# A two-layer encoder on one core: four plain columns and nine pairs in the later feed-forwards, low halves by adding transfers

## The chip, the core and the metric

The kernel runs on one core of a Trainium2 chip. The metric is the time of one execution in device microseconds, as the median of several runs. A core has a matrix engine (TensorE, PE in the rows; PEld is its weight load), a vector engine (VectorE, DVE), an activation engine (ScalarE, ACT), a general engine (GpSimd, POOL) and a sequencer that issues transfers (SyncE, SP). PE writes its sums to PSUM banks; the other engines work on SBUF, and DVE and ACT also read PSUM.

## The reference

Two layers work on 512 tokens of width 1024, in float32. Each layer has a half-step feed-forward, a mixer (a bidirectional state-space scan in the first layer, neighbourhood attention in the second), a second half-step feed-forward, and a gated embedding. So there are four feed-forwards, and they are where the change is:

```python
def swiglu(x, w_gu, w_down):
    g, u = jnp.split(x @ w_gu, 2, axis=-1)
    return (jax.nn.silu(g) * u) @ w_down

for i in range(DEPTH):                       # 2
    h = h + 0.5 * swiglu(rmsnorm(h, ffn1_norm[i]), ffn1_w_gu[i], ffn1_w_down[i])
    ...                                      # h = h + mixer(rmsnorm(h))
    h = h + 0.5 * swiglu(rmsnorm(h, ffn2_norm[i]), ffn2_w_gu[i], ffn2_w_down[i])
    gate = jax.nn.sigmoid(rmsnorm(h, ple_norm[i]) @ ple_w_gate[i])
    h = h + gate * rmsnorm(p[i] @ ple_w_proj[i], ple_post_norm[i])
```

D_MODEL is 1024 and D_FF 2816, which is 22 columns of 128.

## The kernel before

**Two halves per operand.** PE multiplies operands of a shorter float32 format (float32r). Every float32 operand is therefore split into a high half, which is a rounded copy, and a low half, which is the rest, and each product is three matmuls: high by high (L268, or L483 in a pair), high weight by low activation (L271, L484) and low weight by high activation (L272, L485). A weight unit of 128 by 1024 is loaded by SP into a buffer `wr` (L201) and split by `split_raw`: ACT copies it to `wh` (L218), DVE subtracts that copy from it into `wl` (L220). There are four `wr` buffers and three each of `wh` and `wl`. Activations are split in the same way (L286 and L287, with the norm's gain L289 and L290).

**The order of the weights.** `plan` writes out, for the whole program, in which order units are loaded, combined and split. Its items are "u" (a unit that is split as loaded), "g" and "s" (four blocks of a pair are taken, and sums of them are formed by DVE, L240 to L251) and "o" (one of the pair's seven operands is split). `unit` hands PE the next split unit and first tops up the stock to three, so a unit is prepared two units ahead of its use. The framework orders each engine's instructions by a planner of its own; every engine runs its queue in order.

**A feed-forward.** `ffn_order` gives the order of its work. The gate and up projections of the 22 columns come in two kinds. A *plain* column (`gate_up`) is two units, gate and up, each 24 matmuls over all 512 tokens. The other columns come in *pairs* (`block`): for two columns, the two halves of the tokens and two halves of the input width, seven products take the place of eight (a scheme of the Strassen and Winograd kind), each product 24 matmuls over 256 columns. Their activation operands are sums and differences of parts of the normalised input, which `sums` forms in four steps, kk = 0 to 3, each a run of DVE operations (L437 to L468) with copies by ACT between them. These sums need the norm's factor `R`, which is there during the second plain column (in the first feed-forward the third), so they are formed while PE works on the plain columns. The first product reads a part of all four steps, the second needs all four in full. `activate` turns the two PSUM results of a plain column into an entry of `mids`: DVE multiplies both by the factor (L415, L418), ACT applies silu (L416), POOL multiplies (L419), ACT and DVE split (L286, L287).

The columns are grouped in chunks: before, (0, 6) is plain, and (6, 10), (10, 14), (14, 18), (18, 22) are two pairs each. The down projection of a chunk, eight units, is spread between the products of the chunk after it; L546 adds its result to the residual. In the second feed-forward of a layer, the projection of the embedding (`ple_proj`, two units of `w_proj`) stands between the last product and the last chunk's down units, and the gate (`ple`, eight units of `w_gate`) follows.

**Places.** `sums` is called from the loop at the end of `ffn`, after `gate_up`, one step per plain column up to column 3, and the rest at column 4. The first product of the first feed-forward stands at 74.89 us of the span, that of the second at 989.6. POOL issues no transfer in the kernel before.

Of the kernel before, what the change touches and what calls it, by code (L numbers as in the profile page):

```python
# [14 lines left out]
P = 128  # L15
# [32 lines left out]

def ffn_order():

    for f in range(PLAIN):
        yield "plain", f
    for c in range(1, len(CHUNKS)):
        a, b = CHUNKS[c]
        blocks = [(p, i) for p in range(a // 2, b // 2) for i in range(7)]
        d = 0
        for n, (p, i) in enumerate(blocks):
            yield "block", p, i  # L60
            while d < KD and (d + 0.5) * len(blocks) <= KD * (n + 1):
                yield "down", c - 1, d
                d += 1
    yield "between",
    for d in range(KD):
        yield "down", len(CHUNKS) - 1, d


@with_exitstack
def trunk(ctx, tc, A, out):  # L70
# [72 lines left out]
    def plan():  # L143
# [3 lines left out]
        for i in range(stop):  # L147
            l, w = divmod(i, 4)
            if w in (0, 2):
                gu, gw, dn = [A[f"w_{x}{1 + w // 2}"][l] for x in ("gu", "gw", "dn")]  # L150

                def ahead(p, i_):
                    if i_ == 0:
                        yield "g", [gw[p - PLAIN // 2, x, y] for x, y in ((1, 0), (0, 0), (1, 1), (0, 1))]
                    yield "s", (p, i_)

                for what, *a in ffn_order():
                    if what == "plain":
                        for x in range(2):
                            yield "u", gu[a[0], x]  # L160
                            n = 2 * a[0] + x - (2 * PLAIN - 3)
                            if n >= 0:
                                yield from ahead(PLAIN // 2, n)
                    elif what == "block":
                        yield "o", a
                        if a[1] >= 4 and a[0] < NF // 2 - 1:
                            yield from ahead(a[0] + 1, a[1] - 4)
                    elif what == "down":
                        b = CHUNKS[a[0]]
                        yield "u", dn[a[1], :, b[0] * P:b[1] * P]  # L170
                    elif w == 2:
                        for n in range(2):
                            yield "u", A["w_proj"][l, n]
            elif w == 3:
                for n in range(KD):
                    yield "u", A["w_gate"][l, n]
            elif l % 2 == 0:
# [5 lines left out]
            else:  # L183
# [6 lines left out]

    loads = [x for what, a in todo if what in "gu"
             for x in (zip(a, ("wr", "wr", "md", "md")) if what == "g" else [(a, "wr")])]
# [4 lines left out]
    def load_unit():  # L197
# [3 lines left out]
        sy.dma_start(out=raw[:, :n], in_=src)  # L201
        raws.append((raw, n, tag))
        waiting[tag] += 1

    def take():
        if not raws:
            load_unit()
        raw, n, tag = raws.pop(0)
        waiting[tag] -= 1
        return raw, n  # L210

# [3 lines left out]

    def split_raw(raw, n):
        hi = wp.tile([P, 1024], F32R, name=nm("wh"), tag="wh", bufs=3)
        splits.append(s.copy(out=hi[:, :n], in_=raw[:, :n]))  # L218
        lo = wp.tile([P, 1024], F32R, name=nm("wl"), tag="wl", bufs=3)
        v.tensor_sub(out=lo[:, :n], in0=raw[:, :n], in1=hi[:, :n])  # L220
        ready.append((hi, lo))
# [4 lines left out]
    def prep_next():  # L226
# [3 lines left out]
        what, a = item  # L230
        if what == "u":
            split_raw(*take())
        elif what == "g":
            group[:] = [take()[0] for _ in range(4)]
# [141 lines left out]
    def ffn(norm, nxt, between=None, first=None):  # L376
# [150 lines left out]
        made, left = None, [0, 1, 2, 3]  # L527
        for what, *a in ffn_order():
            if what == "plain":
                gate_up(a[0])  # L530
                while left and R[0] is not None:
                    sums(left.pop(0))
                    if a[0] < 4:
                        break
            elif what == "block":
                if between and a == [CHUNKS[-1][0] // 2, 0]:
                    next(between)
# [3 lines left out]
            else:  # L541
                c, d = a
                last = c == len(CHUNKS) - 1
                pt = mm_bank() if last else px_bank()
                gemm(pt, unit(), [mids[f] for f in range(*CHUNKS[c])])
                v.scalar_tensor_tensor(out=h[d], in0=pt, scalar=0.5, in1=h[d], op0=ALU.mult, op1=ALU.add)  # L546
# [754 lines left out]
def prepare(inp):  # L1301
# [11 lines left out]
    for i in (1, 2):  # L1313
        gu = f[f"ffn{i}_w_gu"]
        gu = np.stack([units(gu[l]).reshape(2, NF, P, 1024).transpose(1, 0, 2, 3) for l in range(DEPTH)])
        o[f"w_gu{i}"] = gu[:, :PLAIN]

        gw = gu[:, PLAIN:].reshape(DEPTH, (NF - PLAIN) // 2, 2, 2, P, 2, 512).transpose(0, 1, 3, 5, 4, 2, 6)
        o[f"w_gw{i}"] = gw.reshape(DEPTH, (NF - PLAIN) // 2, 2, 2, P, 1024)
        o[f"w_dn{i}"] = np.stack([units(f[f"ffn{i}_w_down"][l]) for l in range(DEPTH)])  # L1320
    o["w_gate"] = np.stack([units(f["ple_w_gate"][l]) for l in range(DEPTH)])
# [76 lines left out]
```

## Time and profile before

| | |
|---|---|
| median of 3 runs | 2351.93 us (2351.7 to 2353.02) |
| the profiled execution | 2352.96 us, of which the profile's span is 2351.2 us |
| granted PE clock, mean | 0.997 |
| DMA | 265.95 MB, mean 113 GB/s |
| HBM read, written | 253.40 MB, 10.26 MB |

A row of a timeline gives start and duration in us, the engine, the line, the operation, the buffer written and those read, the shape, how many are merged into the row, and in brackets the idle time before it with what ended it. A row of a group view gives line, engine, operation and buffers, the count, then busy us and mean ns of one, then the idle time of the engine just before these instructions with what ended most of it. A row of a line's own view gives the least, median and greatest duration in ns. A row of the transfers gives buffers, issuing queue, count, size and median us from issue to landing. A matmul's row starts when PE takes it; its duration overlaps with the next one's, so PE's time is read from the distance of starts, and the same holds in part for DVE and ACT.

### The profile page before, as it was taken

What the parts mean: (1) busy time and instruction counts of PE and PEld (TensorE: products, weight loads), DVE (VectorE), ACT (ScalarE), POOL (GpSimd) and SP (SyncE); (2) the same over time, 40 slices, a digit from 0 to 9 for tenths busy, and PEclk for the clock granted to TensorE, in tenths of its full rate; (3) what the DMA queues carried; (4) which work ended last, traced back from release to release, by engine and by line L of the source; (5) the groups of instructions that cost most, each with busy time, mean ns of one, the idle gap of its engine ahead of it and who ended that gap; (6) DMA issues with size and microseconds to landing.
All of it is one profiled execution on the core that took longest, in us unless ns stands there. A gap on an engine that the chain in (4) does not pass through costs nothing.

```text
span 2351.2 us, 35169 instructions
## 1 busy us (share of the span) xinstructions
PE 2327.4 (99%) x13810; PEld 2026.6 (86%) x13810; DVE 1805.7 (77%) x2565; ACT 1111.8 (47%) x1819; POOL 353.7 (15%) x309
## 2 busy tenths in 40 slices
PE   9999999999999999999999999999999999999998
PEld 8899998888888888899997889999877888999987
DVE  7878868877777747978877897887778757777767
ACT  5433445755655653433345443334437744334353
POOL 1000001444445551100003110000100011000020
PEclk9999999999999999999999999999999999999999
DMA  5233324544444543323322332332433233333222
GB/s 191 84 101 104 108 72 131 172 138 138 143 136 142 162 162 107 115 84 104 108 86 84 103 115 85 104 108 77 145 121 130 103 100 100 111 108 99 81 81 81
DMA packets 99238, 265.95 MB, mean 113 GB/s; under 512 B 12016, under 2 KB 12912, under 8 KB 99072
## 3 DMA queue, kind: packets, MB, share of 16 engines
q1 hardware_dynamic: 98784, 263.57, 34.8%
q8 instruction: 108, 1.77, 0.3%
q14 instruction: 58, 0.48, 0.1%
q10 hardware_dynamic: 288, 0.14, 0.0%
HBM read 253.40 MB, written 10.26 MB: 112 GB/s over the span
## 4 chain that ended last, share of the span: by engine, by line
PE 90%; DVE 5%; ACT 1%; issue 1%; POOL 1%; DMA 1%; SPq 0%; POOLq 0%; ACTq 0%; DVEq 0%
PE ps L268 19%; PE ps L271 19%; PE ps L272 19%; PE ps L485 9%; PE ps L484 9%; PE ps L483 9%; PE ps L866 1%; DVE wl L220 1%; PE ps L844 1%; PE ps L887 1%; PE ps L800 1%; PE ps L786 1%; PE ps L1172 1%; DVE md L290 1%; DVE md L287 1%
## 5 line engine op out<-in xcount | busy, mean ns | idle before, releaser
L268 PE MATMUL ps<-md,wh 128*128 128x512 f32 x2128 | 838.4, 395 | 2.7 <-ACT md L286 2.1
L272 PE MATMUL ps<-md,wl 128*128 128x512 f32 x2128 | 830.7, 391 | 4.7 <-DVE wl L220 4.7
L271 PE MATMUL ps<-md,wh 128*128 128x512 f32 x2128 | 831.3, 391 | 0.7 <-DVE md L290 0.5
L218 ACT CAST wh<-wr 128x1024 fp32r<-128x1024 f32 (+2 forms) x401 | 358.1, 894 | 521.4 <-PE ps L271 199.9
L220 DVE TENSOR_TENSOR wl<-wr,wh 128x1024 fp32r<-128x1024 f32 (+2 forms) x401 | 429.0, 1070 | 114.1 <-ACT wh L218 85.3
L272 PEld LDWEIGHTS ps<-md,wl 128*128 128x128 f32 x2128 | 400.1, 188 | 90.7 <-DVE wl L220 6.7
L268 PEld LDWEIGHTS ps<-md,wh 128*128 128x128 f32 x2128 | 400.5, 188 | 84.4 <-issue 3.5
L271 PEld LDWEIGHTS ps<-md,wh 128*128 128x128 f32 x2128 | 400.9, 188 | 81.1 <-issue 3.3
L314 POOL TENSOR_TENSOR sq<-sq,sq 128x512 f32<-128x512 f32 x71 | 101.1, 1424 | 1444.8 <-ACT sq L310 1444.0
L218 ACT CAST wh<-md 128x1024 fp32r<-128x1024 f32 x160 | 167.7, 1048 | 297.8 <-PE ps L484 263.0
L483 PE MATMUL ps<-sc,wh 128*128 128x256 f32 x896 | 253.8, 283 | 4.2 <-ACT wh L218 4.2
L485 PE MATMUL ps<-sc,wl 128*128 128x256 f32 x896 | 254.3, 284 | 0.8 <-DVE wl L220 0.8
L484 PE MATMUL ps<-md,wh 128*128 128x256 f32 x896 | 254.1, 284 | 0.0
L485 PE MATMUL ps<-md,wl 128*128 128x256 f32 x896 | 254.1, 284 | 0.0
L484 PE MATMUL ps<-sc,wh 128*128 128x256 f32 x896 | 254.1, 284 | 0.0
L483 PE MATMUL ps<-md,wh 128*128 128x256 f32 x896 | 253.9, 283 | 0.0
L489 DVE TENSOR_TENSOR t<-ps,t 128x512 f32<-128x512 f32 x224 | 151.7, 689 | 129.8 <-PE ps L485 127.9
L220 DVE TENSOR_TENSOR wl<-md,wh 128x1024 fp32r<-128x1024 f32 x160 | 196.5, 1228 | 26.8 <-ACT wh L218 26.7
L483 PEld LDWEIGHTS ps<-sc,wh 128*128 128x128 f32 x896 | 172.1, 192 | 8.4 <-ACT wh L218 4.6
L484 PEld LDWEIGHTS ps<-sc,wh 128*128 128x128 f32 x896 | 172.2, 192 | 3.7
L484 PEld LDWEIGHTS ps<-md,wh 128*128 128x128 f32 x896 | 172.4, 192 | 1.2
L483 PEld LDWEIGHTS ps<-md,wh 128*128 128x128 f32 x896 | 172.4, 192 | 1.2
(207 smaller groups left out, 2859.8 us busy)
## 6 DMA issues: line engine op xcount, KB each, us to landing
wr<-in_w_in_dram SPq DMA_DIRECT2D x65, 512.0 KB, 3.5
wr<-in_w_gw_dram SPq DMA_DIRECT2D x64, 512.0 KB, 4.1
md<-in_w_gw_dram SPq DMA_DIRECT2D x64, 512.0 KB, 5.0
wr<-in_w_dn_dram SPq DMA_DIRECT2D x128, 256.0 KB, 2.7
wr<-in_w_gu_dram SPq DMA_DIRECT2D x44, 512.0 KB, 3.5
hs<-crow SPq DMA_DIRECT2D x64, 256.0 KB, 3.9
wr<-in_w_dn_dram SPq DMA_DIRECT2D x32, 384.0 KB, 3.1
wr<-in_w_qkv_dram SPq DMA_DIRECT2D x24, 512.0 KB, 3.7
```

Of the source, the lines that this page charges most:

```text
L218: splits.append(s.copy(out=hi[:, :n], in_=raw[:, :n]))
L220: v.tensor_sub(out=lo[:, :n], in0=raw[:, :n], in1=hi[:, :n])
L268: m = te.matmul(out=pt, lhsT=hi[:, sl], rhs=part(xp, 0, cols), start=first and k == 0, stop=False)
L271: te.matmul(out=pt, lhsT=hi[:, sl], rhs=part(xp, 1, cols), start=False, stop=False)
L272: te.matmul(out=pt, lhsT=lo[:, sl], rhs=part(xp, 0, cols), start=False, stop=last and k == n - 1)
L287: v.tensor_sub(out=dst[:, 1, :], in0=src, in1=dst[:, 0, :])
L290: v.scalar_tensor_tensor(out=dst[:, 1, :], in0=src, scalar=gain, in1=dst[:, 0, :], op0=ALU.mult, op1=ALU.subtract)
L314: (v if fast else g).tensor_add(out=self.acc, in0=self.acc, in1=q)
L483: te.matmul(out=o, lhsT=hi[:, sl], rhs=xh, start=j == 0 and kk == 0, stop=False)
L484: te.matmul(out=o, lhsT=hi[:, sl], rhs=xl, start=False, stop=False)
L485: te.matmul(out=o, lhsT=lo[:, sl], rhs=xh, start=False, stop=j == 1 and kk == 3)
L489: v.tensor_add(out=k[to], in0=pt, in1=k[other])
```

## The change

The second, third and fourth feed-forwards get their own list of chunks: four plain columns instead of six, then a chunk of three pairs, (4, 10), and the same last three chunks. So each of them has nine pairs instead of eight. The first feed-forward keeps its list. The weights are laid out on the host to match, one array per feed-forward.

`sums` moves: in the later feed-forwards step 0 follows column 1, steps 1 and 2 follow column 2, and step 3 follows column 3, the last. In the first feed-forward there is one step per column from column 2 on, so that step 3 follows column 5, the last, where it stood after column 4.

Plain units, the two units of the projection and the eight of the gate become items "a". Their high half is made as before. Their low half is no longer a subtraction on DVE: ACT writes the negated, rounded copy into `wl` (a second pass over the raw unit), and a transfer issued by POOL reads the unit once more from its array and adds it to `wl`. Units of the down projections, of the mixers and the products of the pairs are split as before.

```diff
-CHUNKS = ((0, 6), (6, 10), (10, 14), (14, 18), (18, 22))
-PLAIN = CHUNKS[0][1]
+FIRST = ((0, 6), (6, 10), (10, 14), (14, 18), (18, 22))
+OTHERS = ((0, 4), (4, 10), (10, 14), (14, 18), (18, 22))
...
                     if what == "plain":
                         for x in range(2):
-                            yield "u", gu[a[0], x]
-                            n = 2 * a[0] + x - (2 * PLAIN - 3)
+                            yield "a", gu[a[0], x]
+                            n = 2 * a[0] + x - (2 * plain - 3)
...
-                            yield "u", A["w_proj"][l, n]
+                            yield "a", A["w_proj"][l, n]
...
-                    yield "u", A["w_gate"][l, n]
+                    yield "a", A["w_gate"][l, n]
...
-    def split_raw(raw, n):
+    def split_raw(raw, n, src=None):
         hi = wp.tile([P, 1024], F32R, name=nm("wh"), tag="wh", bufs=3)
         splits.append(s.copy(out=hi[:, :n], in_=raw[:, :n]))
         lo = wp.tile([P, 1024], F32R, name=nm("wl"), tag="wl", bufs=3)
-        v.tensor_sub(out=lo[:, :n], in0=raw[:, :n], in1=hi[:, :n])
+        if src is None:
+            v.tensor_sub(out=lo[:, :n], in0=raw[:, :n], in1=hi[:, :n])
+        else:
+            s.activation(out=lo[:, :n], in_=raw[:, :n], func=AF.Copy, scale=-1.0)
+            g.dma_start(out=lo[:, :n], in_=src, accum_op=ALU.add)
         ready.append((hi, lo))
...
-        for what, *a in ffn_order():
+        chunks = FIRST if first else OTHERS
+        for what, *a in ffn_order(chunks):
             if what == "plain":
                 gate_up(a[0])
-                while left and R[0] is not None:
+                n = 1 if first else min(a[0], 2)
+                while left and R[0] is not None and n:
                     sums(left.pop(0))
-                    if a[0] < 4:
-                        break
+                    n -= a[0] < chunks[0][1] - 1
```

More of the change, by code (lines that the diff above doesn't have):

```diff
@@ L65, in ffn_order @@
     for d in range(KD):
[L66 removed]
+        yield "down", len(chunks) - 1, d
 @with_exitstack
@@ L189, in trunk @@
     todo = list(plan())
-    loads = [x for what, a in todo if what in "gu"
+    loads = [x for what, a in todo if what in "agu"
              for x in (zip(a, ("wr", "wr", "md", "md")) if what == "g" else [(a, "wr")])]
@@ L1314, in prepare @@
         gu = f[f"ffn{i}_w_gu"]
[L1315 to L1320, printed above, removed]
+        for l in range(DEPTH):
+            k = 2 * l + i - 1
+            plain = (OTHERS if k else FIRST)[0][1]
+            g_ = units(gu[l]).reshape(2, NF, P, 1024).transpose(1, 0, 2, 3)
+            o[f"w_gu{k}"] = g_[:plain]
+            gw = g_[plain:].reshape((NF - plain) // 2, 2, 2, P, 2, 512).transpose(0, 2, 4, 3, 1, 5)
+            o[f"w_gw{k}"] = gw.reshape((NF - plain) // 2, 2, 2, P, 1024)
+            o[f"w_dn{k}"] = units(f[f"ffn{i}_w_down"][l])
     o["w_gate"] = np.stack([units(f["ple_w_gate"][l]) for l in range(DEPTH)])
```

36 lines of the change are left out of this document (20 added, 16 removed).

## The prediction

> **What bounds the kernel now.** I read the page first (engine shares and the chain that ended last), then the busy time of each engine in the stages that the diff touches, then the timelines of PE, DVE, ACT and POOL there, and last the DMA issues.
>
> ```profile
> PE 2327.4 (99%) x13810; PEld 2026.6 (86%) x13810; DVE 1805.7 (77%) x2565; ACT 1111.8 (47%) x1819; POOL 353.7 (15%) x309
> ...
> PE 90%; DVE 5%; ACT 1%; issue 1%; POOL 1%; DMA 1%; SPq 0%; POOLq 0%; ACTq 0%; DVEq 0%
> ```
>
> PE carries the chain for 90% of the span, so what the change takes from PE is worth its full size only where nothing else becomes late. The 77% of DVE is a mean; in the plain stage of the second feed-forward (940 to 990) and in the first one's (44 to 82) it is another engine:
>
> ```profile
> core 0 of [0], span 2351.2 us
> ...
> 940.00:990.00 50.00, 50.00 (x228) 41.56 (x227) 45.70 (x67) 24.61 (x37) 7.80 (x5) 1.00 0.35 115
> 44.00:82.00 38.00, 33.00 (x144) 26.64 (x143) 37.58 (x57) 18.22 (x30) 6.14 (x4) 0.97 0.24 77
> ```
>
> The columns are the stretch, its length, then busy PE, weight load, DVE, ACT, POOL. DVE is busy 45.70 of 50 and 37.58 of 38 us. In the first feed-forward PE already waits for it (33.00 of 38); in the second PE is full, by a hair, as the next part shows.
>
> **The swap on PE.** Two rows one unit apart for each kind of unit, in the second feed-forward:
>
> ```profile
> 946.11 0.39 PE L268 MATMUL ps<-md,wh 128*128 128x512 f32 x1
> ...
> 951.55 0.39 PE L268 MATMUL ps<-md,wh 128*128 128x512 f32 x1
> ```
> ```profile
> 989.63 0.28 PE L483 MATMUL ps<-sc,wh 128*128 128x256 f32 x1
> ...
> 992.51 0.40 PE L268 MATMUL ps<-md,wh 128*128 128x512 f32 x1
> ```
>
> A plain unit is 24 matmuls over 512 columns: 951.55 - 946.11 = 5.44 us. A product of a pair is 24 over 256: 992.51 - 989.63 = 2.88 us. Two plain columns are four units, 21.76 us; a pair is seven products, 20.16 us. Each of the three later feed-forwards swaps one for the other: -1.60 us each, -4.8 us in all. The down units keep their 22 columns of matmuls, the SP queue keeps its number of loads (four per pair as per two columns), and so neither is charged.
>
> **The cover that goes with it.** The three later feed-forwards lose 21.76 us of plain matmuls behind which DVE forms the operand sums (`sums`, four times) that the products read. What DVE does there:
>
> ```profile
> 952.06 1.22 DVE L220 TENSOR_TENSOR wl<-wr,wh 128x1024 fp32r<-128x1024 f32 x1
> 953.20 0.41 DVE L465 TENSOR_TENSOR t<-t,t 128x256 f32<-128x256 f32 x1
> ```
> ```profile
> 979.90 0.69 DVE L415 TENSOR_TENSOR t<-ps,rt 128x512 f32<-128x512 f32 x1
> 980.50 0.68 DVE L418 TENSOR_TENSOR t<-ps,rt 128x512 f32<-128x512 f32 x1
> ```
> ```profile
> 989.22 0.68 DVE L468 TENSOR_TENSOR md<-t,md 128x512 fp32r<-128x512 f32 x1
> ```
> ```profile
> L220 DVE TENSOR_TENSOR wl<-wr,wh 128x1024 fp32r<-128x1024 f32 (+1 forms) x9 | 10.7, 1189 | 2.1 <-PE ps L338 2.1
> ...
> L287 DVE TENSOR_TENSOR md<-t,md 128x512 fp32r<-128x512 f32 x9 | 6.1, 686 | 2.0 <-ACT md L286 1.6
> ...
> L418 DVE TENSOR_TENSOR t<-ps,rt 128x512 f32<-128x512 f32 x5 | 3.4, 688 | 1.5 <-PE ps L272 1.5
> ```
> ```profile
> L437 DVE SCALAR_TENSOR_TENSOR t<-hs,cst,rt x32: 736/746/1792, 44.2 to 1993.7; 128x512 f32<-128x512 f32 x32
> ```
> ```profile
> 981.44 1.55 POOL L419 TENSOR_TENSOR t<-t,t 128x512 f32<-128x512 f32 x1 [10.86 <-ACT t L416]
> ```
>
> The last operation of the last sums starts at 989.22, and PE begins its products at 989.63: no slack. Now the same stage after the change. One L220 costs DVE 953.20 - 952.06 = 1.14 us from start to start, one 512-wide operation 980.50 - 979.90 = 0.60 us. The group view (941.9 to 989.9, the row of nine L220) holds seven of plain units, one of the first product and one of a down unit; the seven go to the transfers: -7 x 1.14 = -8.0 us. The activation of the fifth column (number 4) goes: three 512-wide operations, -1.8 us, and with it one overlap with POOL: of L437's least, median and greatest 736, 746 and 1792 ns the greatest is the one that runs beside POOL's operation (row at 981.44), so -1.0 us. (Number 5's lay behind the sums.) Added ahead of the last sums is the second product's L220, +1.14 us, because with six columns in the second chunk the first down unit comes after two products instead of one. DVE ends the sums at 989.8 - 8.0 - 1.8 - 1.0 + 1.1 = 980.1. PE comes to the first product at 989.63 - 21.76 = 967.9, and to the second product's fourth operand, which needs the last sums, at 967.9 + 2.88 + 9 x 0.12 = 971.8 (0.12 = 2.88 / 24). PE waits 980.1 - 971.8 = 8.3 us. With the swap, 8.3 - 1.6 = +6.7 us in each, +20 us for three.
>
> The ends of this term: of DVE's idle time in that window, 2.0 + 1.5 = 3.5 us by the group rows could be filled by sums moved ahead (the 2.1 before L220 lie before the norm's factor is there), which leaves a stall of 4.8 and +3.2 each. The program does hoist: in the first feed-forward an L437 of the sums ran ahead of the splits that were written before it.
>
> ```profile
> 44.23 1.78 DVE L437 SCALAR_TENSOR_TENSOR t<-hs,cst,rt 128x512 f32<-128x512 f32 x1
> 46.15 2.39 DVE L287 TENSOR_TENSOR md<-t,md 128x512 fp32r<-128x512 f32 x2
> ```
>
> ```profile
> 1243.97 1.05 ACT L218 CAST wh<-wr 128x1024 fp32r<-128x1024 f32 x1 [2.36 <-PE ps L484]
> ...
> 1250.02 1.14 ACT L286 CAST md<-sq 128x512 fp32r<-128x512 f32 x2
> ```
>
> Upward, ACT gets a second pass per plain unit (1.05 us, row at 1243.97; the row at 1250.02 is used further down) ahead of the copies that the sums wait for, and the L220 that filled DVE's waits inside the sums are gone: four of 1 us, so +10.7 each. Part of the idle time filled and part of this lost, about even, leaves 6.7.
>
> The trace shows no transfer issued by POOL, so what that does to DVE is unknown. [...]
>
> **The adding transfers.** 52 units take them: 8 in the first feed-forward (12 less the four begun by hand), 8 in each other, 4 of the projection, 16 of the gate. Each takes 1.14 us from DVE and gives ACT one more pass, POOL an issue, and the DMA engines 512 KB more.
>
> ```profile
> wr<-in_w_gu_dram SPq DMA_DIRECT2D x44, 512.0 KB, 3.5
> t<-ydram SPq DMA_DIRECT2D x6, 256.0 KB, 6.5
> ```
>
> A low half is now ready after ACT's copy, ACT's negated copy, the issue and the landing: 1.05 + 1.05 + an issue between nothing and 1.6 (one POOL operation in front, the row at 981.44) + a landing between 3.5 and 6.5, the fastest load of that size and the slowest landing of the table: 5.6 to 10.2 us. I take 1 and 5, 8.1 us, the middle of both, since a landing that also adds is nearer to neither row. Its time is two units of PE, 10.88 us, as three low-half buffers allow. So inside the plain units it is hidden behind PE's matmuls; uncovered it would cost up to 10.2. The new waits: ACT's negated copy waits for the buffer, with the gate's activations and the copies of the sums queued behind it, for which DVE waits; POOL's issue waits for that copy, with the next product of L419 behind it, for which ACT and then DVE wait. Both stand in the +10.7. [...]
>
> The first feed-forward keeps its six columns and only gains the transfers:
>
> ```profile
> 79.94 0.58 PE L483 MATMUL ps<-sc,wh 128*128 128x256 f32 x1 [4.19 <-ACT wh L218]
> ...
> 81.55 0.58 PE L485 MATMUL ps<-sc,wl 128*128 128x256 f32 x1 [0.82 <-DVE wl L220]
> ```
> ```profile
> L220 DVE TENSOR_TENSOR wl<-wr,wh 128x1024 fp32r<-128x1024 f32 x5 | 6.1, 1217 | 0.0
> ```
>
> PE stands 4.19 + 0.82 = 5.0 us (the brackets are the idle time before the row). Of the five L220 in that window one is the first product's; four go, 4.6 us of a DVE that has no idle time: -4.5 us. Ends: -5.0 (all) and +0.5, if the last sums, which now stand behind column 5, are kept there.
>
> At the projection and the gate the lead is shorter:
>
> ```profile
> 1250.68 0.50 PE L268 MATMUL ps<-md,wh 128*128 128x512 f32 x1 [1.05 <-ACT md L286]
> ```
> ```profile
> 1287.15 0.50 PE L272 MATMUL ps<-md,wl 128*128 128x512 f32 x1 [2.04 <-DVE wl L220]
> ```
> ```profile
> 1281.85 1.99 ACT L218 CAST wh<-wr 128x1024 fp32r<-128x1024 f32 x2
> ```
>
> Projection: the first low half is there at 1243.97 + 8.1 = 1252.1, wanted at about 1251.1 (two matmuls after 1250.68), and L286, for which PE waits, stands behind two more ACT passes: +1.5 us, from 0 to +3.2 (landing 6.5). Gate: 1281.85 + 8.1 = 1290.0 against 1287.15 is +2.8, less what the freed L220 give back to DVE behind it, at most the 2.0 us of the present stall: +1 us, from -2.0 to +5. Two of each: +5 us.
>
> **Sum.** 20 - 4.5 + 5 = +20.5 us. The profiled execution is 2352.96 us (span 2351.2), 1.0 above the median of 2351.93; the difference set on the median gives 2372.
>
> **Rivals.** *Faster: the sums fit.* The 3.5 us of DVE's idle time are filled, the first down unit (12 matmuls of 0.227, 2.7 us) is put ahead of the second product, and the sums run clear of POOL, which is worth another 1.0 us in each of the two overlaps left: 8.3 - 3.5 - 2.7 - 2.0 = 0.1, and nothing waits. Then -4.8 - 5.0 and at best 2 x -2.0 at the gate: -14 us, 2338. The hoisted L437 speaks for it; against it the L418 row, five activations whose 1.5 us of waiting for PE was not filled by sums. It decides from a stall under 1.6 us. *Slower still: the transfers are late.* If a landing takes 11 us, the chain is 14.1 and a unit comes every (14.1 + 5.44) / 3 = 6.5 us instead of 5.44: +1.07 us for the 24 units of the first feed-forward and the gate, +26 us on top, 2398; in the other three it hides in the stall for the sums. It decides from a landing of 7.8 us. [...] *No change:* stalls of 3 us each (+4 in all), -4.5 and nothing at projection and gate: 2352.
>
> **Numbers.** This kernel can be told from no change at about 0.2%, 4.7 us. Forecast 2372 (from 2357 to 2392 on its own): 0.56; late transfers 0.14; sums fit 0.21; no change 0.09. Faster 0.21, same 0.09, slower 0.70. The range leaves out the tail of each end rival: 2341 to 2399.
>
> **What would show it.** L268 and its two fellows fall by 96 matmuls each, the three 256-wide lines rise by 168 each. PE should show a wait of 4 to 12 us at the first two products of the last three feed-forwards, released by DVE's L468 or L220 or by ACT, and DVE busy without a gap there; the wait in the first feed-forward about 1 us. Wrong if no wait stands there (DVE then started the sums before 946), if plain units wait for the transfer, or if the adding transfers land over 7.8 us after issue.

## The result and the profile after

The changed kernel takes 2393.07 us (median of four, 2389.58 to 2394.76) against 2351.9 us: ratio 1.0172, 95% interval 1.0155 to 1.019. That is slower by 41 us, where 20 were forecast: the sign was right, the size was half. The profiled execution is 2391.99 us, its span 2390.2.

The page of the kernel after: the engines, two DMA queues (packets, MB, share of 16 engines' span), and four rows of the issues (last column: us from issue to landing):

```profile
PE 2335.6 (98%) x14026; PEld 2040.7 (85%) x14026; DVE 1783.6 (75%) x2549; ACT 1171.0 (49%) x1883; POOL 386.4 (16%) x355
...
q1 hardware_dynamic: 98784, 263.57, 33.9%
q0 software_dynamic: 7488, 27.27, 6.4%
...
wr<-in_w_gu_dram SPq DMA_DIRECT2D x32, 512.0 KB, 5.0
wl<-in_w_gu_dram POOLq DMA_DIRECT2D x32, 512.0 KB, 8.0
...
wl<-in_w_gate_dram POOLq DMA_DIRECT2D x16, 512.0 KB, 7.6
...
wl<-in_w_proj_dram POOLq DMA_DIRECT2D x4, 512.0 KB, 6.6
```

DVE's busy time fell by 22 us (from 1805.7) and PE's rose by 8; neither is 41 us. The adding transfers land 6.6 to 8.0 us after their issue (the medians of the three arrays; single ones take 5.5 to 12.1), where 3.5 to 6.5 had been allowed. What PE waited for (us in total, times, longest):

```profile
PE ps L492 <- ACT md L455: 14.8, 4, 4.6
PE ps L281 <- DMA wl<-in_w_gate_dram: 14.3, 3, 6.7
PE ps L281 <- DMA wl<-in_w_gu_dram: 7.0, 4, 3.3
PE ps L281 <- DMA wl<-in_w_proj_dram: 4.4, 2, 2.4
PE ps L494 <- DVE wl L224: 4.0, 6, 1.2
```

Two families stand there. The first and the last row are the products waiting for the sums and for the low halves of their own weights, which DVE forms between the sums (L492 to L494 are the pair's three matmul lines, L455 a copy in `sums`, L224 is before's L220): forecast. The three in the middle are low halves that a transfer had not yet landed (25.7 us): forecast as hidden in the plain columns and as 5 us at projection and gate. Of the 25.7 us, 16.7 stand at the first unit of the projection and of the gate (2.0, 2.4, 6.7 and 5.6), and 9.0 in five waits further on: at the second and fourth unit of a feed-forward, the fifth transfer of the first one and the gate's last unit. The products' wait in the second feed-forward:

```profile
969.59 0.38 PE L494 MATMUL ps<-sc,wl 128*128 128x256 f32 x1 [1.16 <-DVE wl L224]
...
971.67 0.39 PE L494 MATMUL ps<-sc,wl 128*128 128x256 f32 x1 [0.28 <-DVE wl L224]
...
977.34 0.58 PE L492 MATMUL ps<-md,wh 128*128 128x256 f32 x1 [4.57 <-ACT md L455]
978.09 0.58 PE L493 MATMUL ps<-md,wh 128*128 128x256 f32 x1 [0.17 <-DVE md L456]
...
978.68 0.41 PE L492 MATMUL ps<-sc,wh 128*128 128x256 f32 x1
978.90 0.41 PE L493 MATMUL ps<-sc,wh 128*128 128x256 f32 x1
...
984.17 0.28 PE L493 MATMUL ps<-sc,wh 128*128 128x256 f32 x1
984.29 0.28 PE L494 MATMUL ps<-sc,wl 128*128 128x256 f32 x1
```

By the brackets PE stands 6.2 us; by the distance of starts, less a matmul's own time, 7.1. Then something that the prediction has no term for: the rows at 978.68 and 978.90 stand 0.22 us apart, those at 984.17 and 984.29 0.12. After the wait PE runs at half its clock. The windows show it (PEclk is the third number from the end):

```profile
940.00:990.00 50.00, 43.82 (x207) 37.12 (x206) 41.50 (x63) 21.82 (x34) 7.12 (x6) 0.90 0.40 103
44.00:82.00 38.00, 35.76 (x165) 29.03 (x164) 34.92 (x54) 21.89 (x34) 10.49 (x9) 1.00 0.70 188
968.00:985.00 17.00, 10.82 (x55) 9.41 (x54) 15.00 (x24) 6.76 (x12) 1.58 (x1) 0.80 0.29 105
```

In the first row PE is busy 43.82 of 50 us (50.00 before) at a clock of 0.90 (1.00), and DVE 41.50 (45.70); in the third, around the wait, the clock is 0.80. In the second, the first feed-forward, PE went from 33.00 to 35.76 of 38 us. The trace's record of the granted clock has seven stretches at 0.50, each 3.41 or 6.83 us long, which begin inside a wait or less than 1 us behind it. The length of the wait does not settle it alone: two of them follow waits of 1.9 and 3.3 us, and beside the projection's waits of 2.0 and 2.4 us the clock stayed at 1.00.

A table of stages shows where the 39 us of the span (2390.2 - 2351.2) lie. Each number is how much more (us) a stage took than in the kernel before, read from the timelines between the same instructions: the norm's first small matmul at a stage's start, and the last DVE operation of the second chunk's down units (L556) at the end of a feed-forward's part. "Gate" runs from there to the next norm, or to the end, and so holds what the entry to the third feed-forward costs too. The other kernels are those of the experiments.

| stage | after | transfers only | columns only | no add | entries on DVE | entries, six columns | entries, early down | columns, filled |
|---|---|---|---|---|---|---|---|---|
| feed-forward 1 | -5.4 | -2.7 | -1.9 | -6.4 | -3.2 | -3.6 | -4.7 | -2.0 |
| mixer | +0.4 | -0.6 | +1.7 | -0.9 | -0.6 | -0.7 | -0.4 | +1.8 |
| feed-forward 2 | +13.6 | +5.1 | +9.4 | +8.8 | +9.6 | +4.5 | +4.8 | +8.4 |
| gate, entry to 3 | +8.8 | +8.8 | +0.1 | +1.3 | +0.8 | +2.3 | +0.9 | 0.0 |
| feed-forward 3 | +7.3 | +5.8 | +10.3 | +8.0 | +11.9 | +4.4 | +10.0 | +8.5 |
| mixer | -0.5 | -0.8 | -0.8 | -0.5 | -0.8 | -0.8 | -0.8 | -0.8 |
| feed-forward 4 | +10.3 | +3.7 | +9.4 | +7.9 | +13.6 | +6.8 | +4.7 | +8.4 |
| gate | +4.5 | +8.1 | -0.1 | 0.0 | +0.2 | +0.2 | +0.2 | -0.1 |
| span | +39.0 | +27.4 | +28.1 | +18.1 | +31.5 | +13.1 | +14.6 | +24.2 |

My theory from this: three costs add up. The sums come late in the later feed-forwards (as forecast), PE loses its clock after these waits, and the adding transfers land too late wherever a stage begins. The rivals: one of the two edits does all the damage; the half clock is only a sign of the waits and costs nothing itself; every adding transfer is late, not only those at a stage's entry; and what is slow in the transfers is POOL's issue, not the add.

### The profile page after: what moved, and what is told of

The parts are those of the page before. It is cut to its first block, busy times and chain, and to the rows that moved or that the text cites. A ratio compares the mean times of both kernels' runs of the same rounds, so it can differ in the third digit from the quotient of the medians.

```text
span 2390.2 us, 35793 instructions
## 1 busy us (share of the span) xinstructions
PE 2335.6 (98%) x14026; PEld 2040.7 (85%) x14026; DVE 1783.6 (75%) x2549; ACT 1171.0 (49%) x1883; POOL 386.4 (16%) x355
## 5 line engine op out<-in xcount | busy, mean ns | idle before, releaser
L281 PE MATMUL ps<-md,wl 128*128 128x512 f32 (+1 forms) x2032 | 797.0, 392 | 26.4 <-DMA wl<-in_w_gate_dram 14.3
L277 PE MATMUL ps<-md,wh 128*128 128x512 f32 (+1 forms) x2032 | 804.2, 396 | 0.0
L280 PE MATMUL ps<-md,wh 128*128 128x512 f32 (+1 forms) x2032 | 795.2, 391 | 0.0
L281 PEld LDWEIGHTS ps<-md,wl 128*128 128x128 f32 x2032 | 383.5, 189 | 112.2 <-DMA wl<-in_w_gate_dram 15.6
L277 PEld LDWEIGHTS ps<-md,wh 128*128 128x128 f32 x2032 | 384.2, 189 | 77.0 <-issue 3.5
L280 PEld LDWEIGHTS ps<-md,wh 128*128 128x128 f32 x2032 | 384.0, 189 | 75.6 <-issue 3.3
L224 DVE TENSOR_TENSOR wl<-wr,wh 128x1024 fp32r<-128x1024 f32 (+2 forms) x343 | 355.9, 1038 | 104.9 <-ACT wh L221 80.7
L492 PE MATMUL ps<-md,wh 128*128 128x256 f32 x980 | 279.3, 285 | 14.8 <-ACT md L455 14.8
L494 PE MATMUL ps<-sc,wl 128*128 128x256 f32 x980 | 279.2, 285 | 4.0 <-DVE wl L224 4.0
L493 PE MATMUL ps<-md,wh 128*128 128x256 f32 x980 | 279.3, 285 | 0.5 <-DVE md L456 0.5
L494 PE MATMUL ps<-md,wl 128*128 128x256 f32 x980 | 278.8, 284 | 0.0
L493 PE MATMUL ps<-sc,wh 128*128 128x256 f32 x980 | 278.6, 284 | 0.0
L492 PE MATMUL ps<-sc,wh 128*128 128x256 f32 x980 | 278.2, 284 | 0.0
L224 DVE TENSOR_TENSOR wl<-md,wh 128x1024 fp32r<-128x1024 f32 x175 | 213.6, 1221 | 21.4 <-ACT wh L221 21.3
L492 PEld LDWEIGHTS ps<-md,wh 128*128 128x128 f32 x980 | 189.5, 193 | 17.2 <-ACT md L455 15.9
L494 PEld LDWEIGHTS ps<-sc,wl 128*128 128x128 f32 x980 | 189.1, 193 | 6.0 <-DVE wl L224 6.0
L492 PEld LDWEIGHTS ps<-sc,wh 128*128 128x128 f32 x980 | 189.3, 193 | 3.6
L493 PEld LDWEIGHTS ps<-sc,wh 128*128 128x128 f32 x980 | 189.1, 193 | 3.6
```

What stands on the lines that cost most here:

```text
L277: m = te.matmul(out=pt, lhsT=hi[:, sl], rhs=part(xp, 0, cols), start=first and k == 0, stop=False)
L280: te.matmul(out=pt, lhsT=hi[:, sl], rhs=part(xp, 1, cols), start=False, stop=False)
L281: te.matmul(out=pt, lhsT=lo[:, sl], rhs=part(xp, 0, cols), start=False, stop=last and k == n - 1)
L492: te.matmul(out=o, lhsT=hi[:, sl], rhs=xh, start=j == 0 and kk == 0, stop=False)
L493: te.matmul(out=o, lhsT=hi[:, sl], rhs=xl, start=False, stop=False)
L494: te.matmul(out=o, lhsT=lo[:, sl], rhs=xh, start=False, stop=j == 1 and kk == 3)
```

## The experiments

The kernel before ran beside all of them: 2353.27 us beside the transfers, the columns, the spare matmuls in the changed kernel and the first feed-forward alone; 2352.74 beside the two kernels with entries on DVE and the two with an earlier down unit; 2352.76 beside the other four. Kernels with the transfers vary by 3 to 10 us between runs, so their differences are read by stages too.

**Transfers only.** Six plain columns everywhere, sums in their old places; the low halves by adding transfers (64 of them, since the later feed-forwards have twelve plain units again, where the changed kernel has 52).

```diff
-OTHERS = ((0, 4), (4, 10), (10, 14), (14, 18), (18, 22))
+OTHERS = FIRST
...
-                n = 1 if first else min(a[0], 2)
-                while left and R[0] is not None and n:
+                while left and R[0] is not None:
                     sums(left.pop(0))
-                    n -= a[0] < chunks[0][1] - 1
+                    if a[0] < 4:
+                        break
```

> The kernel before with adding transfers for all plain units, the projection and the gate, but six plain columns and the old places of the sums everywhere. Theory A (three causes add up: the sums come late in the three later feed-forwards, low halves land late where the lead is short, and after every longer wait PE runs at half its clock for 3.4 to 6.8 us): the first feed-forward keeps its gain of about 5, the gates cost 4 to 5 each, the first plain units of the later feed-forwards 2 to 5 each, so 10 to 18 us over before, 2362 to 2370. Rival B (the four columns are the whole loss, the transfers are harmless): 5 to 6 us under before, 2346. Rival C (the transfers are nearly the whole loss): 30 us or more over before.

Measured: 2383.01 us (2380.47 to 2385.7), ratio 1.0126 (1.0113 to 1.014): +30 us, above the 2362 to 2370 that my theory gave. PE's waits:

```profile
PE ps L281 <- DMA wl<-in_w_gate_dram: 14.9, 3, 6.6
PE ps L281 <- DMA wl<-in_w_gu_dram: 11.9, 7, 3.2
```

Nothing else waits for as much. The transfers alone, put where DVE's subtraction did no harm, cost as much as three quarters of the whole loss; a kernel with the old columns and the old cover still pays for them.

**Columns only.** The new columns and the sums' new places, the low halves by DVE as before.

```diff
         if what == "a":
-            split_raw(*take())
+            split_raw(*take()[:2])
```

> The changed kernel with every low half formed by the subtraction on DVE again, four columns and nine pairs kept. Theory A: no wait for a transfer, but three or four more subtractions of 1.14 us lie ahead of the last sums: waits of 10 to 12 us in front of the products and about 3 us of half clock behind them, less 1.6 for the swap, 11 to 14 us in each of three, so 2386 to 2394. Rival B: the same or more than the changed kernel, 2393 and up. Rival C: under 2367, since the columns cost little by themselves.

Measured: 2382.06 us (2378.96 to 2383.51), ratio 1.012 (1.0107 to 1.0134): +29 us, 9.4 to 10.3 in each later feed-forward, nothing at the gates; 11 to 14 each had been expected. Each part alone is slower by about 30 us and both together by 41. Two reasons are likely, and no run separates them: the waits for low halves partly fall into time in which DVE's late sums would have held PE anyway, and the transfers take seven subtractions from DVE in each of these stages. The first feed-forward gains 1.9 us here, from the new place of the last sums alone: the place was worth a gain, not the loss that the prediction allowed as its end.

**Spare matmuls in the wait.** The changed kernel, and 36 matmuls of 256 columns in front of the first product's fourth operand in the later feed-forwards; their sums go to a bank that nobody reads.

```diff
                 for kk in range(4):
+                    if not first and p == OTHERS[1][0] // 2 and i == 0 and j == 0 and kk == 3:
+                        spare = px_bank()
+                        for _ in range(FILLERS):                     # 36
+                            te.matmul(out=spare[:, :HT], lhsT=hi[:, :P], rhs=xs[0][0][0], start=True, stop=True)
```

> The changed kernel with 36 more matmuls over 256 columns (into a spare bank that nothing reads) where PE waits for the last sums in the three later feed-forwards. 36 x 0.12 = 4.3 us of work that fits in the wait of 4.7. Theory A: PE does not idle long enough to lose its clock, the 6.8 us of half clock behind each of these waits go, and the time falls by 2 to 3 us in each, 2384 to 2387. Rival: the slow matmuls behind the wait have another cause (operands that come late one by one): no change or up to 4 us more.

Measured: 2389.97 us (2382.85 to 2392.31), ratio 1.0159 (1.0144 to 1.0175). The clock in the second feed-forward's wait:

```profile
968.00:985.00 17.00, 15.34 (x114) 14.26 (x113) 16.18 (x23) 7.37 (x11) 1.59 (x1) 1.00 0.39 141
```

PEclk is 1.00 where it was 0.80: added work brings the clock back. The time is only 3 us lower, above the 2384 to 2387 expected, and the intervals overlap: by itself this does not settle what the half clock costs, since kernels with the transfers vary by more than that from run to run. So the same was done without the transfers:

> The four columns and nine pairs alone (low halves by DVE's subtraction as before), with 36 spare matmuls of 256 columns put where PE waits for the last sums, in the first product of each later feed-forward; their result is not used. They take 36 x 0.12 = 4.3 us of PE, which lies inside the wait if the wait is 4.3 us or more. Theory A (the waits of 2.0 + 1.5 + 3.5 us cost more than their length, because the granted clock halves for 10 to 14 us after them): the half-clock stretches at the products vanish, each later feed-forward costs 4 to 6 us less than the 9.4 to 10.3 of the columns alone, and the time is 12 to 17 us below the 2382 of the columns alone: 2365 to 2370. Theory B (the half clock is a result of the thin load and not a cost of its own): no gain, 2380 to 2384, or up to 13 us more if the spare matmuls lie outside the wait.

Measured: 2377.24 us (2376.44 to 2377.61), ratio 1.01 (1.0085 to 1.0116), 4.8 us below the columns alone; by the stages 1.0, 1.8 and 1.0 us in the three feed-forwards. The gain was expected at 12 to 17, so this prediction of mine failed too. The rows say why. First the columns alone:

```profile
978.97 0.58 PE L492 MATMUL ps<-md,wh 128*128 128x256 f32 x1 [3.20 <-ACT md L455]
...
980.53 0.41 PE L493 MATMUL ps<-sc,wh 128*128 128x256 f32 x1
980.75 0.41 PE L494 MATMUL ps<-sc,wl 128*128 128x256 f32 x1
```

And filled (the lines stand five higher):

```profile
978.95 0.39 PE L497 MATMUL ps<-md,wh 128*128 128x256 f32 x1 [0.42 <-ACT md L456]
979.70 0.39 PE L498 MATMUL ps<-md,wh 128*128 128x256 f32 x1 [0.37 <-DVE md L457]
...
981.91 0.50 PE L282 MATMUL ps<-md,wl 128*128 128x512 f32 x1 [0.28 <-DVE wl L225]
```

The last sums arrive at 978.97 and 978.95: spare work on PE does not move them. Behind that point PE is quicker at full clock, and then waits again for DVE (0.37, 0.28). The half clock is real, and taking most of it away saves 1 to 2 us at each of these waits. In the columns alone the stretch is 10.24 us long here, but it begins at 973.01, and only 4.28 us of it (978.97 to 983.25, granted clock 0.50) lie behind the wait: at full clock that would be 2.1 us less. Of these 1.0 came, and the two waits for DVE, which sets the pace there, take most of the rest. With the spare matmuls a stretch of 3.41 us is left, from 973.07 on, ahead of the last sums.

**First feed-forward only.** Before's columns and places of the sums (the edit shown under *Transfers only*); only the first feed-forward's plain units take transfers.

```diff
-                            yield "a", gu[a[0], x]
+                            yield ("a" if i == 0 else "u"), gu[a[0], x]
...
-                            yield "a", A["w_proj"][l, n]
+                            yield "u", A["w_proj"][l, n]
...
-                    yield "a", A["w_gate"][l, n]
+                    yield "u", A["w_gate"][l, n]
```

> The kernel before with adding transfers for the eight plain units of the first feed-forward alone, nothing else changed. Theory A: the wait for the sums there goes from 5 us to about 1, with the half clock behind it: 4 to 6 us under before, 2346 to 2348. Rival: the gain of the first feed-forward came from the new place of the last sums: no change from before.

Measured: 2348.75 us (2346.47 to 2351.68), ratio 0.9983 (0.9974 to 0.9992): -4.5 us. The one stage where PE waited for a DVE without idle time is the one stage that gains: 3.8 us in the profiled execution, with nothing of the kind elsewhere (at most 0.6 in a mixer).

**Without the add.** POOL's transfer as it is, less `accum_op`; the kernel leaves out the add, so these low halves hold the whole unit.

```diff
-            g.dma_start(out=lo[:, :n], in_=src, accum_op=ALU.add)
+            g.dma_start(out=lo[:, :n], in_=src)
```

> Leaves out the add: POOL's transfer copies the unit into the low half, so the low halves of the plain, projection and gate units hold the whole unit; every instruction and every issue stays. The question is what makes a landing take 8.0 us where SP's loads of the same 512 KB take 3.5. Theory A (the add in the transfer, which also showed 89.7 engine-us per MB against 49.2): landings fall to 4 to 5 us, the waits of the first plain units and of the gate for the low half fall from 25.7 us in all to under 10, and the time falls by 8 to 15 us from the changed kernel's 2393, to 2378 to 2385. [...]

Measured: 2371.07 us (one run), 22 us below the changed kernel and below the 2378 to 2385 that was expected. The transfers:

```profile
q0 software_dynamic: 7488, 27.27, 3.4%
...
wl<-in_w_gu_dram POOLq DMA_DIRECT2D x32, 512.0 KB, 5.1
...
wl<-in_w_gate_dram POOLq DMA_DIRECT2D x16, 512.0 KB, 4.3
```

The issue on POOL (ns, least, median and greatest) and the landings of all 52, first with the add, then without:

```profile
L227 POOL DMA_DIRECT2D wl<-in_w_gu_dram x32: 853/875/996, 19.3 to 1993.6; - x32
...
DMA to landing us min/median/max: 5.5/7.7/12.1
```
```profile
L227 POOL DMA_DIRECT2D wl<-in_w_gu_dram x32: 527/536/672, 18.8 to 1978.3; - x32
...
DMA to landing us min/median/max: 3.7/4.6/8.0
```

The same packets and bytes as above take 3.4% of 16 engines' span instead of 6.4, and land in 5.1 and 4.3 us instead of 8.0 and 7.6. POOL and its queue are the same in both, so it is the add that makes a landing slow. A small part is the issue itself, which is 0.34 us longer with the add (0.875 against 0.536); the rest is the transfer, which takes 1.9 times the engine time (6.4 x 2390.2 over 3.4 x 2369.3). SP's loads of the same array land sooner too, in 3.5 us where the changed kernel has 5.0. With a landing of 5 us, the value that the prediction took, PE's waits for low halves fall from 25.7 to 8.7 us by the list of waits, and the gate stages cost +1.3 and 0.0. And the later feed-forwards, with transfers that cost next to nothing, still lose 7.9 to 8.8 us each: this is the price of the columns with DVE relieved.

**Negated copy first.** ACT's two passes exchanged, so that the transfer is issued one pass sooner.

```diff
-        splits.append(s.copy(out=hi[:, :n], in_=raw[:, :n]))
...
             s.activation(out=lo[:, :n], in_=raw[:, :n], func=AF.Copy, scale=-1.0)
             g.dma_start(out=lo[:, :n], in_=src, accum_op=ALU.add)
+            splits.append(s.copy(out=hi[:, :n], in_=raw[:, :n]))
```

> The changed kernel with ACT's two passes over a plain unit exchanged: the negated copy first, so that the adding transfer is issued one pass (1.05 us) sooner and the high half is ready one pass later. Theory A (the first plain units and the gate wait for the end of the chain copy, negated copy, issue, landing): each wait for a low half, nine of them by the list of waits, shortens by up to 1.05 us, less where PE now waits for the high half instead: 3 to 8 us less than the changed kernel, 2385 to 2390. Theory B (the transfers queue behind one another, so that an earlier issue lands no earlier): within 3 us of 2393.

Measured: 2396.22 us (2391.37 to 2396.66), ratio 1.0177 (1.0163 to 1.0191). No gain. The list of PE's waits has 14.9 us for the gate's low halves, where it had 14.3. At the two entries to the gate the issue came 0.7 us sooner after ACT's first pass, not 1.05 (1293.30 - 1291.58 against 1293.93 - 1291.53 at the first), because POOL was still in an addition of the norm (1291.82, 1.54 us); and the landing took longer, 8.5 and 7.9 us where it had taken 8.0 and 6.9.

**The entries on DVE.** The changed kernel, but with DVE's subtraction for the units that stand first behind another stage: the first column of the later feed-forwards, the projection, and the gate's first two units.

```diff
-                            yield "a", gu[a[0], x]
+                            yield ("u" if i and not a[0] else "a"), gu[a[0], x]
...
-                            yield "a", A["w_proj"][l, n]
+                            yield "u", A["w_proj"][l, n]
...
-                    yield "a", A["w_gate"][l, n]
+                    yield ("u" if n < 2 else "a"), A["w_gate"][l, n]
```

> The changed kernel, but the units that stand first behind a stage of other work get their low half from DVE's subtraction again: the first column of the later feed-forwards (two units), the projection's two and the gate's first two. The others keep their transfers. Theory A (a landing of 8 us is hidden by two units of 5.44 us, but not at an entry, where the stock of three was filled behind short down units or other stages): the waits for low halves go, which are worth 21 us by the run without the add; two subtractions of 1.14 us return to DVE ahead of each later feed-forward's sums and cost between nothing and 2.3 us each: 2370 to 2378. Theory B (every transfer is late, wherever it stands): the second column and the gate's third unit wait in their place, 2386 or more.

Measured: 2380.76 us (2374.83 to 2384.52), ratio 1.011 (1.0093 to 1.0127): 12 us less than the changed kernel, between the 2370 to 2378 of the one theory and the 2386 of the other. Neither has the whole of it. The gates cost nothing any more (+0.8 and +0.2 in the table), although 12 of their 16 units still take transfers: at the gate it is the entry. In the feed-forwards the wait moved to the second column. The entry to the third one, ACT, then POOL, then PE:

```profile
1343.70 0.72 ACT L298 ACTIVATE md<-hs,cst 128x512 fp32r<-128x512 f32 x1 [2.90 <-DVE hs L610]
...
1344.86 1.03 ACT L221 CAST wh<-wr 128x1024 fp32r<-128x1024 f32 x1
1345.80 0.71 ACT L608 ACTIVATE t<-t 128x256 f32<-128x256 f32 x2
1346.42 1.04 ACT L226 ACTIVATE wl<-wr 128x1024 fp32r<-128x1024 f32 x1
```
```profile
1347.87 0.88 POOL L227 DMA_DIRECT2D wl<-in_w_gu_dram  x1 [1.47 <-DVE hs L610]
```
```profile
1356.81 0.79 PE L281 MATMUL ps<-md,wl 128*128 128x512 f32 x1 [3.32 <-DMA wl<-in_w_gu_dram]
```

The copy of the unit stands in ACT's queue behind the norm's activation, which waits 2.90 us for DVE; the gate's activations part the two passes; the issue follows at 1347.87, and the unit lands 8.9 us later, at 1356.8. From the first pass that makes 1356.81 - 1344.86 = 12 us, against the 8.1 us forecast, with 8.6 us of work left on PE (1356.81 - 3.32 - 1344.86). The two units of lead are there only for a unit whose passes ACT reaches at once.

The same entries with six plain columns and the old places of the sums:

> The transfers alone (six plain columns and eight pairs in every feed-forward, sums in their old places), with the same entry units on DVE's subtraction. Theory A (transfers cost nothing where the lead is two units, and relieve a DVE that nobody waits for): the 30 us that the transfers alone cost go, and what is left is the first feed-forward's gain: 2346 to 2352. Theory B (every transfer is late): 2370 or more.

Measured: 2367.15 us (2366.3 to 2369.88), ratio 1.0063 (1.0048 to 1.0078): half of the transfers' 30 us went, the half that lay at gates and projection. PE still waits 11.0 us for low halves in the plain columns; the expectation of 2346 to 2352 failed there for the reason just shown.

**The first down unit sooner.** The kernel with the entries on DVE, and one down unit ahead of the second product.

```diff
-            while d < KD and (d + 0.5) * len(blocks) <= KD * (n + 1):
+            while d < KD and ((d + 0.5) * len(blocks) <= KD * (n + 1)
+                              or chunks[0][1] == 4 and c == 1 and n == 0 and d == 0):
```

> The kernel with DVE's subtraction at the entries, and the first down unit (12 matmuls, 2.7 us) placed ahead of the second product, as my rival with fitting sums had it. Theory A (PE waits 7 us there and any work put into the wait is saved): 2.7 us less in each later feed-forward than without it, 8 us in all. Theory B (PE's queue already draws two matmuls of that unit forward, and the wait ends with DVE's last sums plus what DVE then owes to the second product; DVE also gets the down unit's subtraction earlier, 0.5 us): no more than 1 us each, within 3 us of the kernel without it, on either side.

Measured: 2368.69 us (2366.09 to 2375.44), ratio 1.0072 (1.0055 to 1.0088): 12 us less than without it, where 8 was the most expected. DVE's queue in the second feed-forward shows what more was won. With the entries alone:

```profile
967.86 1.22 DVE L224 TENSOR_TENSOR wl<-md,wh 128x1024 fp32r<-128x1024 f32 x1
...
969.60 1.22 DVE L260 TENSOR_TENSOR md<-md,md 128x1024 f32<-128x1024 f32 x1
...
971.93 2.41 DVE L446 SCALAR_TENSOR_TENSOR t<-hs,cst,rt 128x512 f32<-128x512 f32 x2
```

With the down unit ahead of the second product:

```profile
965.67 0.69 DVE L224 TENSOR_TENSOR wl<-wr,wh 128x512 fp32r<-128x512 f32 x1
...
968.15 2.41 DVE L446 SCALAR_TENSOR_TENSOR t<-hs,cst,rt 128x512 f32<-128x512 f32 x2
...
973.24 1.22 DVE L224 TENSOR_TENSOR wl<-md,wh 128x1024 fp32r<-128x1024 f32 x1
...
975.32 1.22 DVE L260 TENSOR_TENSOR md<-md,md 128x1024 f32<-128x1024 f32 x1
```

The second product's low half (L224 on `md`) and the pair's next difference (L260) now stand behind the first operations of the last sums (L446), not ahead; a half-width split took their place. That is the +1.14 us for the second product's split which the prediction counted ahead of the sums, and L260 beside it, which it did not count. PE gets work for the wait and the wait itself gets shorter. Alone in the changed kernel the edit did the same in the feed-forwards, in one run:

> The changed kernel with only the first down unit ahead of the second product. Same question as with the entries mended, one look: theory A 2.7 us less in each later feed-forward in the stage from the sums to the end of the first pairs; theory B within 1 us of the changed kernel's stage.

Measured: 2384.89 us, 8 us below the changed kernel; the three feed-forwards cost 7.6, 6.5 and 5.3 us where they cost 13.6, 7.3 and 10.3.

**A version that beats both.** The kernel before; in the first feed-forward alone the adding transfers (negated copy first) and the last sums behind column 5.

> The kernel before with three edits, all in the first feed-forward: its eight plain units take adding transfers, ACT writes their negated copy first, and step 3 of the sums follows column 5. Transfers there alone gave -4.5 us, step 3's place alone -1.9, both together in the changed kernel -5.4 at the end of that feed-forward. Theory A (the waits left of 1.62 + 0.91 + 1.5 us are partly for low halves, which an earlier issue shortens): -5.5 to -8 us against the kernel before. Theory B (what is left is DVE's work): -5.4, as in the changed kernel, within 0.5.

Measured: 2346.45 us (2344.98 to 2347.86), ratio 0.9971 (0.9959 to 0.9982): 6.3 us faster than the kernel before, too close to both expectations to tell them apart. In its first feed-forward PE waits twice:

```profile
53.54 0.50 PE L282 MATMUL ps<-md,wl 128*128 128x512 f32 x1 [0.88 <-DMA wl<-in_w_gu_dram]
79.12 0.39 PE L493 MATMUL ps<-md,wh 128*128 128x256 f32 x1 [1.09 <-ACT md L456]
```

That is 2.0 us instead of the 5.0 of before; and the first feed-forward ends 6.1 us sooner.

## Why the prediction was half right

**The swap and the wait for the sums: right.** L281's group has 2032 matmuls where L272's had 2128, 96 fewer. The wait was forecast at 8.3 us in each feed-forward, between 4.8 and some 12; it is 7.1 by starts in the second, with DVE busy through it and the releasers of the kind that was named: ACT's copy (L455) and DVE (L456 in the sums, L224); the last operation of the sums, before's L468, is not among them. The place was another, too: the sum had PE wait at the second product's fourth operand, at 971.8, but the 4.57 us stand at the first product's fourth operand (977.34), which needs only the first results of the last sums (L455 and L456); PE came to the second product's at 981.24 and did not wait. Where the transfers land soon (no add), a later feed-forward costs 7.9 to 8.8 us against the +6.7 of the sum. So the +20 us was mis-sized by about 5 us. The wait was no longer than forecast (7.1 - 1.6 = 5.5 where 6.7 was taken), so what is missing lies beside it. Part of that is the half clock, which the prediction left out although the kernel before's window of 44 to 82 showed 0.97 beside PE's waits: 1.0 to 1.8 us each, by the columns with spare matmuls. The rest was not taken apart.

**The first feed-forward: right.** -4.5 forecast, -5.4 in the changed kernel; the bound of +0.5, for the last sums' later place, pointed the wrong way: that place alone gains 1.9, in the one profile of the columns alone.

**The adding transfers: the step that failed.** "I take 1 and 5": the landing was set between two rows of plain loads, 3.5 and 6.5 us, and an adding transfer was outside both, at 8.0. The run without the add gives the 5 us that was assumed, and takes 22 us off the time; with the add a transfer takes 1.9 times the engine time. The second assumption failed as well: "Its time is two units of PE, 10.88 us". That is the lead in the middle of a row of plain units. For the gate the sum had a shorter one, 5.3 us (1287.15 - 1281.85); at its first low half it was 3.7 (1301.97 - 6.71 - 1291.53):

```profile
1290.38 0.72 ACT L298 ACTIVATE md<-hs,cst 128x512 fp32r<-128x512 f32 x1 [2.94 <-DVE hs L556]
...
1291.53 1.04 ACT L221 CAST wh<-wr 128x1024 fp32r<-128x1024 f32 x1
1292.48 1.05 ACT L226 ACTIVATE wl<-wr 128x1024 fp32r<-128x1024 f32 x1
```
```profile
1293.93 0.90 POOL L227 DMA_DIRECT2D wl<-in_w_gate_dram  x1 [0.63 <-ACT wl L226]
```
```profile
1301.97 0.80 PE L281 MATMUL ps<-md,wl 128*128 128x512 f32 x1 [6.71 <-DMA wl<-in_w_gate_dram]
```

ACT reaches the unit at 1291.53, behind an activation that waits for the down units' result; the landing is at 1302.0, 8 us after the issue. So the chain took 10.4 us (1301.97 - 1291.53) in place of 8.1, and PE stands 6.71 us, against the 2.04 of before. The table's two gate stages, with projection and the entry to the third feed-forward in them, took 13.3 us more in place of 5, and 1.3 without the add; the three later feed-forwards took 6.5 us more than without the add (31.2 against 24.7), in place of nothing. Projection: the list of waits has 4.4 us in two where 2.1 stood before, +1.2 each for the +1.5 forecast. Term by term, the sum's 20 - 4.5 + 5 for columns, first feed-forward and entries came out as 24.7 - 5.4 + 13.3, and the 6.5 in the plain columns had been put at nothing: 39.1, where the span grew by 39.0.

**The rivals.** "The transfers are late" named 2398 and the right engine, and its point of decision, 7.8 us, is where the landing came out, but its mechanism was another: a rate of one unit in 6.5 us, +1.07 us for each of 24 units. No such rate limit shows: with the entries on DVE the gate's 12 transfers keep up, but for one wait of 0.3 us. The loss is a few long waits, two thirds of it (16.7 of 25.7 us) at entries. "The sums fit" was right in one thing, that a down unit ahead of the second product helps, by more than its 2.7 us; its other terms did not come.

**What stays open.** How the 41 us divide between sums and landing cannot be given to a microsecond: each run has its own landings, waits of the one kind cover waits of the other, and the kernel without the add ran once. Why the landings spread from 5.5 to 12.1 us, and why a transfer that was issued 0.7 us sooner took about as much longer to land, is not shown.

## What to carry to other kernels

Work taken off an engine is worth something only in the stage where another engine waits for it: here the same transfers gained 4.5 us in the first feed-forward and lost some 30 in the rest of the kernel. A latency that is hidden "two units ahead" has to be set against the lead at the entry of each stage, where the stock was filled behind other work in an engine's queue (here ACT stood 2.94 us ahead of the gate's first copy, whose unit was loaded), and not in the middle of a row. When operations are dropped to relieve a full queue, what stands in that queue ahead of the critical operation counts for as much as its length.

## What the hardware showed beside the forecast

An adding transfer of 512 KB issued by POOL lands in 6.6 to 8.0 us (medians; 5.5 to 12.1 singly), and the same transfer without the add in 4.3 to 5.1 (3.7 to 8.0). Its issue keeps POOL busy for about 0.87 us with the add and 0.54 without. The three landings over 10 us (11.1, 12.1 and 10.6) belong to transfers issued 1.9 us after another one; two others issued so landed in 8.1 and 9.7 us. In the changed kernel PE's granted clock halves in stretches of 3.41 and 6.83 us beside waits of 1.9 to 6.7 us. The price of a stretch, 1.0 to 1.8 us in each feed-forward of the columns alone, is less than half its length (10.24 us in the second) because part of it passes while PE still waits (3.20 us there), and because the engine that PE waited for is then late again (0.37 and 0.28 us).
